# Multiplying the last experts' column factors into their weights, the final norm's products on VectorE, and holding one weight fetch behind the first gather

## The chip, the cores and the metric

The kernel runs on one core of one Trainium2 chip, in one launch. The metric is the device time of that launch in microseconds. A program on one core has one span: from its first to its last instruction. TensorE is called PE here, VectorE DVE, ScalarE ACT, GpSimd POOL; SP is the engine that issues most of the DMAs. Each of them works its own queue of instructions strictly in the order that was fixed when the kernel was built.

## The reference, cut to what matters

One layer of a hybrid backbone on 1024 tokens of width 1024, then a final RMSNorm. What bears on the change is its end, the mixture of 16 experts and the norm:

```python
x = x + mod_l[2] * token_mixer_out(zl, lat_grid, lp, ml_l)
x = x + mod_l[5] * hier_moe(modulate(rmsnorm(x, norm2_w[l]), mod_l[3], mod_l[4]), lp)
...
return rmsnorm(x, norm_f_w)

def hier_moe(h, lp):            # top-1 group of 4, then top-2 experts inside it
    ...
    hg = jnp.einsum("nd,edh->neh", t, lp["moe_w_gate"])
    hu = jnp.einsum("nd,edh->neh", t, lp["moe_w_up"])
    a = jax.nn.silu(hg) * hu * combine[..., None].astype(t.dtype)
    return jnp.einsum("neh,ehd->nd", a, lp["moe_w_down"]).reshape(B, L, D)
```

Each token goes to two of the 16 experts with a weight for each, and the sum of the two outputs is multiplied, column by column, by `mod_l[5]`, which is one row of 1024 factors for all tokens.

## The kernel before

**Stage out.** For each tile t of 128 tokens, `product` makes the mixer's output on PE and adds it to the residual, `transpose` and `logits` make the router's logits, `norm(t)` (L1580 to L1586) scales the tile's rows by their root mean square on ACT (L1584), adds the shift row on POOL (L1585) and writes the rows to `h2d` in DRAM; the last tile is done in two halves of 512 columns. `route` and `rank` are some twenty small DVE instructions per tile that end in the index lists `idx` (L1662) of each expert.

**Stage experts.** The jobs are the 16 experts, in a fixed order, `jobs[0]` to `jobs[15]`. For each: `exp_load` gathers the expert's rows in two halves of 112 by indirect DMAs on POOL's queue (L1672, 458 KB each); `exp_fetch` loads six weight tiles of 512 KB through SP's queue (four for gate and up, two for down); `exp_weights` splits each tile into a high part, cast on ACT (L1703), and a low part, subtracted on DVE or, for three tiles of the first job, on POOL (L1705); `exp_rows` or, for the first job, `exp_rows_first` transposes the rows on PE (L1721, L1738) and splits them (`split`, L215 on ACT and L216 on DVE); `exp_up` runs the products (three matmuls for each product of split parts, L230 to L232), then silu, the product with the up part (`a`, L1759) and its split (`ah`, `al`); `exp_down` runs the second products and evicts each half of 112 rows with one DVE instruction `y = p * weight * mod5` (L1777), where `weight` is the token's weight (gathered from `wd` in DRAM on POOL's queue, L1677) and `mod5` the row of column factors.

For the first 13 jobs y is added to `sum` in DRAM by an indirect DMA (L1681). The last three, the late ones, keep their sum on chip: `late_load` gathers their rows of `sum`, `exp_down` adds y (L1783), and `late` normalises the half (`late_norm`: squares, square root, reciprocal, then a product with the row `nf`) and scatters it to the output (L1681 again). All rows of `sum` are also read back (`rest_load`, eight tiles) and normalised by `rest_norm` for the tokens that no late expert touches: squares on ACT (L1900), an inverse square root by small DVE instructions on all eight tiles at once (L1902 and L1182 to L1187), then for tiles 0 to 3 one DVE instruction (L1907), and for tiles 4 to 7 a scale on ACT (L1909) and a product on POOL (L1910). `late` for job 13 also uses ACT and POOL (L1935, L1936), for jobs 14 and 15 DVE (L1934). The late scatters wait for all eight tiles of `rest_norm` to have been written, since they replace rows of these.

**The order.** A scheduler orders the instructions of each engine when the kernel is built, by the order in which the program states them and by its own estimate of when each is ready; `issue_after(i)` puts what follows behind instruction i on i's engine, `high_priority` ahead. In `stage_experts`, the casts of the first job stand behind `self.scaled`, the last ACT instruction of `norm`, and its DVE low parts behind `self.last`, the instruction that makes `idx`. A semaphore wait between queues is made by `sync_dep`. `rest_norm`'s DVE part stands behind `al` of job 14, `late` of job 13 behind the silu and `al` of job 15.

Of the kernel before, what the change touches and what calls it, by code (L numbers as in the profile page):

```python
# [8 lines left out]
F32 = mybir.dt.float32  # L9
F32R = mybir.dt.float32r  # L10
I32 = mybir.dt.int32
AF = mybir.ActivationFunctionType
ALU = mybir.AluOpType
# [17 lines left out]
HALF = CAP // 2  # L31
# [133 lines left out]
class Prog:  # L165
# [1289 lines left out]
    def stage_out(self):  # L1455
        nc = self.nc
# [25 lines left out]
        for dst, n, step, ch in ((self.ios, CAP, 1, 0), (tok, 8, 128, 1)):  # L1482
            i = self.t("O", "h", 2, I32, (128, n))
# [3 lines left out]
        i = self.t("O", "h", 2, F32, (128, 128))  # L1487
# [11 lines left out]
        gate, sh2, sc2 = (self.row_bc("O", f"row{i}", i) for i in (0, 1, 2))  # L1499
        self.x1 = []  # L1500
        for t in range(8):
            x = self.t("X", "x", 8)
# [4 lines left out]
        rs = self.t("O", "h", 2, F32, (128, 8, 20))  # L1507
# [3 lines left out]
        prep, rstd, sel = {}, {}, {}  # L1511

        def job(e):
            i = ORDER.index(e)
            k = i - NE + LATE
            extra = {} if k < 0 else dict(out=lambda h: self.oidx[:HALF, 2 * k + h:2 * k + h + 1],
                                                late=lambda h: self.yl[k * CAP + HALF * h:k * CAP + HALF * h + HALF, :])
            return dict(extra, e=e, pool="E", w=("X", "x", 8) if i % 2 else ("EW", "w", 6), n=HALF, halves=2, last=e == ORDER[-1],
                        idx=lambda h: self.idx[:, NE * h + e:NE * h + e + 1],
                        wgu=lambda i: A["w_gu"][e, i].rearrange("p k h -> p (k h)"),  # L1520
                        wdn=lambda k: A["w_dn"][e, :, k, :],
                        dst=lambda h: self.sidx[:HALF, NE * h + e:NE * h + e + 1])

        jobs = [job(e) for e in ORDER]
# [55 lines left out]
        def norm(t):  # L1580
            n = D if t < 7 else D // 2
            for a in range(0, D, n):
                h = hs[t][:, a:a + n]
                self.scaled = nc.scalar.activation(h, h, AF.Copy, scale=rstd[t])  # L1584
                nc.gpsimd.tensor_add(h, h, sh2[:, a:a + n])  # L1585
                nc.sync.dma_start(self.h2d[128 * t:128 * t + 128, a:a + n], h)  # L1586

        hs, ss, hT = {}, {}, {}
        split_m(0), split_m(1)
        for t in range(9):  # L1590
            if t < 8:
                product(t, 0)
            if t == 0:
                q = self.ps("ph", (128, 20))
# [93 lines left out]
            self.take(w[h], self.wd, j["idx"](h))  # L1688
        j["weight"] = lambda h: w[h][:, e:e + 1]

    def exp_fetch(self, j):
        j["m"] = [self.load(*j["w"], j["wgu"](i) if i < 4 else j["wdn"](i - 4)) for i in range(6)]

    def exp_weights(self, j, engines="vvvvvv", hi_after=None, lo_after=None):
        nc = self.nc
        pool = j["pool"]
        after = lambda i: self.tc.issue_after(i.ins) if i is not None else ExitStack()
        j["gu"], j["dn"], j["pins"] = [], [], []
        for i, m in enumerate(j["m"]):
            tag, bufs = ("g", 5) if i < 4 or i == 5 and j["last"] else ("d", 3)  # L1700
            mh, ml = (self.t(pool, tag + x, bufs, F32R, m.shape) for x in "hl")
            with after(hi_after):
                copied = nc.scalar.copy(mh, m)  # L1703
            with after(lo_after):
                lo = (nc.vector if engines[i] == "v" else nc.gpsimd).tensor_sub(ml, m, mh.bitcast(F32))  # L1705
            j["pins"].append((copied, lo))
            j["gu" if i < 4 else "dn"].append((mh, ml))
# [21 lines left out]
    def exp_rows_first(self, j):  # L1729

        n = j["n"]
        xh, xl = (self.t(j["pool"], x, 2, F32R, (128, 8, 2 * n)) for x in ("xh", "xl"))
        for h in range(2):
            p = self.ps("pb", (128, 2, 512))
            for q in range(2):
                for k in range(4):
                    kk = 4 * q + k
                    self.nc.tensor.transpose(p[:, q, n * k:n * k + n], j["rows"][h][:, 128 * kk:128 * kk + 128],  # L1738
                                             self.ident[:n, :n])
                s = slice(4 * q, 4 * q + 4), slice(n * h, n * h + n)  # L1740
                self.split(xh[:, s[0], s[1]], xl[:, s[0], s[1]], p[:, q, :4 * n].rearrange("p (k n) -> p k n", n=n))
        j["x"] = xh, xl

    def exp_up(self, j, between=None):
# [19 lines left out]
    def exp_down(self, j):  # L1764
        nc = self.nc
        pool, n, w = j["pool"], j["n"], j["n"] * j["halves"]
        ah, al = j["a"]
        j["y"] = []
        for h in range(j["halves"]):
            p = self.ps("pb", (128, 2, 512))  # L1770
            for k in range(2):
                for b in range(2):
                    s = slice(k * w + h * n, k * w + h * n + n)
                    c = slice(512 * b, 512 * b + 512)
                    self.mm3(p[:n, b, :], ah[:, s], al[:, s], j["dn"][k][0][:, c], j["dn"][k][1][:, c], k == 0, k == 1)
            y = self.t(*j["tags"][h])[:n] if "tags" in j else self.t(pool, "y", 2, F32, (n, D))
            nc.vector.scalar_tensor_tensor(y, p[:n].rearrange("p a b -> p (a b)"), j["weight"](h), self.mod5[:n],  # L1777
                                           op0=ALU.mult, op1=ALU.mult)
            j["y"].append(y)
            if "late" in j:  # L1780
                if "tags" not in j:
                    nc.sync.dma_start(j["late"](h), y)
                nc.vector.tensor_add(j["sum"][h], j["sum"][h], y)  # L1783
            elif self.in_loop:
                self.put(self.sum, j["dst"](h), y, compute_op=ALU.add)
            else:
                self.put_sum(j, h, y)
# [23 lines left out]
    def stage_experts(self):  # L1811
        nc = self.nc
# [8 lines left out]
        jobs = self.jobs  # L1821
# [8 lines left out]
        for e in range(NE):  # L1830
            if e + 2 < NE:
                self.exp_load(jobs[e + 2])
                self.exp_fetch(jobs[e + 2])

            between = {0: lambda: self.exp_rows(jobs[1]), NE - 3: lambda: self.exp_down(jobs[NE - 4]),
                       NE - 2: lambda: self.exp_down(jobs[NE - 3])}.get(e)
# [7 lines left out]
            if e == NE - 2:  # L1844
                with self.tc.issue_after(jobs[-1]["pins"][3][1].ins):
                    self.late_load(jobs[-2], "X", "x", 8)
                    self.late_load(jobs[-1], "X", "x", 8)
                self.rest_norm(jobs[-1]["pins"][2][0], jobs[-2]["silu"], jobs[-2]["al"])
            if e == NE - 1:
                with self.tc.issue_after(jobs[e]["silu"].ins), self.tc.issue_after(jobs[e]["al"].ins):  # L1850
                    self.late(jobs[-3], "gg")
                jobs[-2]["tags"] = (("X", "x", 8),) * 2
            if e and not between:
                self.exp_down(jobs[e - 1])
# [5 lines left out]
            if 4 <= e < 12:  # L1860
                t = e - 4
# [28 lines left out]
            self.after_puts(self.nc.sync.dma_start(x, self.sum[128 * t:128 * t + 128, :]))  # L1890
            self.xr.append(x)

    def rest_norm(self, act, act2, dve):

        nc = self.nc
        ss = self.t("V", "ss", 1, F32, (128, 8))
        for a, i in ((0, act), (4, act2)):
            with self.tc.issue_after(i.ins):
                for t in range(a, a + 4):
                    nc.scalar.activation(self.scratch, self.xr[t], AF.Square, accum_out=ss[:, t:t + 1])  # L1900
        with self.tc.issue_after(dve.ins):
            nc.vector.tensor_scalar(ss, ss, 1.0 / D, EPS, op0=ALU.mult, op1=ALU.add)  # L1902
            r = self.rsqrt("V", "rs", ss, 8)
            for t in (0, 4, 1, 5, 2, 6, 3, 7):
                x = self.xr[t]
                if t < 4:
                    nc.vector.scalar_tensor_tensor(x, x, r[:, t:t + 1], self.nf, op0=ALU.mult, op1=ALU.mult)  # L1907
                else:
                    nc.scalar.activation(x, x, AF.Copy, scale=r[:, t:t + 1])  # L1909
                    nc.gpsimd.tensor_mul(x, x, self.nf)  # L1910
                self.rest_out.append(nc.sync.dma_start(self.out[128 * t:128 * t + 128, :], x))

    def late(self, j, eng="vv"):
        for h in range(2):
            last = self.late_norm("E", HALF, j["sum"][h], self.scratch[:HALF], eng[h])
        with self.tc.issue_after(last.ins):
            for h in range(2):
                self.late_out(j["sum"][h], j["out"](h))
# [5 lines left out]
            self.after_puts(self.take(x, self.sum, j["idx"](h)))  # L1924
            j["sum"].append(x)

    def late_norm(self, pool, n, x, o, eng="v"):
        nc = self.nc
        r = self.t(pool, "r", 3, F32, (n, 1))
        nc.scalar.activation(o, x, AF.Square, accum_out=r)  # L1930
        nc.scalar.activation(r, r, AF.Sqrt, bias=self.eps[:n], scale=1.0 / D)
        nc.vector.reciprocal(r, r)
        if eng == "v":
            return nc.vector.scalar_tensor_tensor(x, x, r, self.nf[:n], op0=ALU.mult, op1=ALU.mult)  # L1934
        nc.scalar.activation(x, x, AF.Copy, scale=r)  # L1935
        return nc.gpsimd.tensor_mul(x, x, self.nf[:n])  # L1936

    def late_out(self, x, idx):
        i = self.put(self.out, idx, x)
# [195 lines left out]
```

## Time and profile before

| | us |
|---|---|
| median of 3 runs (lowest, highest) | 1715.55 (1713.96, 1719.74) |
| the profiled execution, whole time | 1713.86 |
| its span | 1712.1 |
| PE busy in the span | 1573.3 |
| DVE, ACT, POOL busy | 1194.5, 680.2, 333.6 |

A timeline row gives the start in us from the span's start, the duration in us, the engine, the line, the operation, what it writes and reads, the count of merged instructions, and in brackets how long the engine had been idle before and what ended that. The matmuls' ends are modelled, so a busy PE is not PE at its peak.

### The profile page before, as it was taken

Reading aid. Unit: us, or ns where it says so; the run is one execution under the profiler, and the core shown is the slowest. Engines: PE = TensorE matmul, PEld = TensorE weight load, DVE = VectorE, ACT = ScalarE, POOL = GpSimd, SP = SyncE. Lnnn points to the kernel's source line nnn. Section 1 sums busy time; section 2 is a strip of 40 time slices with the busy share of each in tenths; the row PEclk is TensorE's granted clock in tenths of the full one; section 3 lists DMA queues with packets and bytes.
Section 4 is the critical chain, followed back from the end, with each engine's and each line's share of the span. In section 5 each row is a group of like instructions: output and inputs, shape, how many; then the busy total and the mean of one; then the engine's idle time right before and its main releaser. Section 6 shows DMA issues by size and latency. Waiting matters only on the chain. (4 is left out here: it accounts for less than half of the span.)

```text
span 1712.1 us, 22676 instructions
## 1 busy us (share of the span) xinstructions
PE 1573.3 (92%) x8473; PEld 1300.0 (76%) x8473; DVE 1194.5 (70%) x1831; ACT 680.2 (40%) x1029; POOL 333.6 (19%) x288
## 2 busy tenths in 40 slices
PE   3999999699999999999999888899999969999992
PEld 1477777588877877888788777778888869999991
DVE  5678776898996437888643998864255467777766
ACT  4464555343330123444424433232133354544553
POOL 0000000000000001000001300026623354565636
PEclk9999999899999999999999999999999979999996
DMA  7533466222244436777443532486563389999974
GB/s 266 173 125 134 172 243 221 105 83 97 92 143 189 157 117 201 261 241 267 165 161 110 164 104 94 163 302 202 170 223 112 135 242 248 312 282 287 268 210 164
DMA packets 124355, 317.03 MB, mean 185 GB/s; under 512 B 18009, under 2 KB 40529, under 8 KB 124242
## 3 DMA queue, kind: packets, MB, share of 16 engines
q1 hardware_dynamic: 111562, 278.72, 47.2%
q0 software_dynamic: 10496, 32.36, 7.8%
q10 hardware_dynamic: 2184, 4.47, 0.7%
q8 instruction: 68, 1.11, 0.3%
q14 instruction: 45, 0.37, 0.1%
HBM read 226.49 MB, written 89.01 MB: 184 GB/s over the span
## 5 line engine op out<-in xcount | busy, mean ns | idle before, releaser
L230 PE MATMUL gp<-ht,wh 128*128 128x512 f32 x784 | 310.9, 397 | 17.9 <-ACT z L708 17.6
L232 PE MATMUL gp<-ht,wl 128*128 128x512 f32 x784 | 310.8, 396 | 0.0
L231 PE MATMUL gp<-ht,wh 128*128 128x512 f32 x784 | 309.8, 395 | 0.0
L230 PEld LDWEIGHTS gp<-ht,wh 128*128 128x128 f32 x784 | 148.7, 190 | 51.6 <-ACT z L708 18.4
L232 PEld LDWEIGHTS gp<-ht,wl 128*128 128x128 f32 x784 | 148.7, 190 | 32.2 <-issue 2.2
L231 PEld LDWEIGHTS gp<-ht,wh 128*128 128x128 f32 x784 | 148.5, 189 | 31.6 <-issue 1.2
L230 PE MATMUL pb<-xh,gh 128*128 128x224 f32 x512 | 142.5, 278 | 0.0
L231 PE MATMUL pb<-xl,gh 128*128 128x224 f32 x512 | 141.6, 277 | 0.0
L232 PE MATMUL pb<-xh,gl 128*128 128x224 f32 x512 | 141.0, 275 | 0.0
L723 DVE SCALAR_TENSOR_TENSOR u<-z,hy_cw,u 128x945 f32<-128x945 f32 (+2 forms) x96 | 115.3, 1221 | 3.6 <-ACT u L715 1.6
L215 ACT CAST wh<-w 128x1024 fp32r<-128x1024 f32 x57 | 59.8, 1050 | 138.5 <-PE gp L231 95.5
L230 PEld LDWEIGHTS pb<-xh,gh 128*128 128x128 f32 x512 | 99.3, 194 | 0.3 <-ACT xh L215 0.2
L231 PEld LDWEIGHTS pb<-xl,gh 128*128 128x128 f32 x512 | 99.3, 194 | 0.1
L232 PEld LDWEIGHTS pb<-xh,gl 128*128 128x128 f32 x512 | 99.3, 194 | 0.0
L216 DVE TENSOR_TENSOR wl<-w,wh 128x1024 fp32r<-128x1024 f32 x57 | 71.1, 1248 | 39.3 <-ACT wh L215 39.2
L723 DVE SCALAR_TENSOR_TENSOR u<-z,ml_cw,u 128x945 f32<-128x945 f32 (+2 forms) x64 | 77.7, 1221 | 3.8 <-ACT u L715 2.4
L216 POOL TENSOR_TENSOR ml<-m,mh 128x512 fp32r<-128x512 f32 x24 | 35.6, 1484 | 191.2 <-ACT mh L215 187.7
L708 ACT ACTIVATE z<-gp,bh 128x512 f32<-128x512 f32 x46 | 31.5, 685 | 100.1 <-PE gp L232 91.7
L864 POOL MEMSET z<- 128x1024 f32 x1 | 1.0, 962 | 312.2 <-DVE u L723 312.2
L1705 DVE TENSOR_TENSOR gl<-x,gh 128x1024 fp32r<-128x1024 f32 x33 | 40.8, 1240 | 29.9 <-ACT gh L1703 29.9
L1681 POOL DMA_INDIRECT sum<-y,sidx x26 | 42.9, 1650 | 79.4 <-DVE y L1777 76.1
L1444 DVE SCALAR_TENSOR_TENSOR g<-g,pb 128x1024 f32<-128x1024 f32 x16 | 19.5, 1221 | 53.9 <-PE pb L232 53.9
(610 smaller groups left out, 4011.2 us busy)
## 6 DMA issues: line engine op xcount, KB each, us to landing
w<-in_ada_rest SPq DMA_DIRECT2D x32, 512.0 KB
w<-in_w_gu SPq DMA_DIRECT2D x32, 512.0 KB
x<-in_w_gu SPq DMA_DIRECT2D x32, 512.0 KB
w<-in_w_gate SPq DMA_DIRECT2D x24, 512.0 KB
g<-gd SPq DMA_DIRECT2D x24, 512.0 KB
gd<-z SPq DMA_DIRECT2D x23, 512.0 KB
r<-in_ada_in SPq DMA_DIRECT2D x16, 512.0 KB
pd<-ft SPq DMA_DIRECT2D x32, 256.0 KB
```

Source lines behind the costliest of these rows:

```text
L215: self.copied = nc.scalar.copy(hi, src)
L216: return (nc.vector if eng == "v" else nc.gpsimd).tensor_sub(lo, src, hi.bitcast(F32))
L230: mm(ps, lh, rh, start=start, stop=False)
L231: mm(ps, lh, rl, start=False, stop=False)
L232: mm(ps, ll, rh, start=False, stop=stop)
L708: return lambda s, p: self.nc.scalar.activation(z[:, s], p, func, bias=bias, scale=scale)
L723: last = nc.vector.scalar_tensor_tensor(ui[:, r0:r1, c0:c1], zi[:, r0 + dy:r1 + dy, c0 + dx:c1 + dx], taps[:, i:i + 1], ui[:, r0:r1, c0:c1 ...
L864: nc.gpsimd.memset(zt, 0.0)
L1444: nc.vector.scalar_tensor_tensor(g, g, 1.0, p, op0=ALU.add, op1=ALU.mult)
L1681: return self.nc.gpsimd.indirect_dma_start(out=out, out_offset=bass.IndirectOffsetOnAxis(ap=ix, axis=0), in_=src, in_offset=None, **kw)
L1705: lo = (nc.vector if engines[i] == "v" else nc.gpsimd).tensor_sub(ml, m, mh.bitcast(F32))
```

## The change

It has two places.

At the end: the six down tiles of the three late jobs are multiplied by `mod5` on DVE before they are split, so that the eviction needs the token's weight alone. The sum is then updated straight from PSUM by one DVE instruction, `sum = p * weight + sum`, and y, which only the overflow path and `yl` need, is written by an ACT copy with a scale. `rest_norm` becomes two calls of four tiles each, with an inverse square root for each, and all eight products are DVE instructions; the first call's DVE part stands behind the low part of tile 4 of job 15, the second behind the last product of the first. `late_norm` has the DVE form alone. No POOL product is left there.

At the start of the experts: `norm(7)` becomes one DVE instruction per half instead of ACT and POOL, and `self.scaled` is not assigned for that tile. The six weight fetches of `jobs[2]` wait for `jobs[0]["in"]`, the last split of the first job's rows.

```diff
@@ stage_out, norm
-                self.scaled = nc.scalar.activation(h, h, AF.Copy, scale=rstd[t])
-                nc.gpsimd.tensor_add(h, h, sh2[:, a:a + n])
+                if t == 7:
+                    nc.vector.scalar_tensor_tensor(h, h, rstd[t], sh2[:, a:a + n], op0=ALU.mult, op1=ALU.add)
+                else:
+                    self.scaled = nc.scalar.activation(h, h, AF.Copy, scale=rstd[t])
+                    nc.gpsimd.tensor_add(h, h, sh2[:, a:a + n])
@@ exp_fetch, exp_weights, exp_rows_first
-    def exp_fetch(self, j):
-        j["m"] = [self.load(*j["w"], j["wgu"](i) if i < 4 else j["wdn"](i - 4)) for i in range(6)]
+    def exp_fetch(self, j, after=None):
+        j["m"] = []
+        for i in range(6):
+            m = self.t(*j["w"])
+            d = self.nc.sync.dma_start(m, j["wgu"](i) if i < 4 else j["wdn"](i - 4))
+            if after is not None:
+                self.sync_dep(d, after, "the first rows go ahead")
+            j["m"].append(m)
...
+            if "late" in j and i >= 4:
+                nc.vector.tensor_mul(m, m, self.mod5)
...
-                self.split(xh[:, s[0], s[1]], xl[:, s[0], s[1]], p[:, q, :4 * n].rearrange("p (k n) -> p k n", n=n))
+                j["in"] = self.split(xh[:, s[0], s[1]], xl[:, s[0], s[1]], p[:, q, :4 * n].rearrange("p (k n) -> p k n", n=n))
@@ exp_down
-            nc.vector.scalar_tensor_tensor(y, p[:n].rearrange("p a b -> p (a b)"), j["weight"](h), self.mod5[:n],
-                                           op0=ALU.mult, op1=ALU.mult)
...
             if "late" in j:
+                nc.vector.scalar_tensor_tensor(j["sum"][h], p, j["weight"](h), j["sum"][h], op0=ALU.mult, op1=ALU.add)
+                nc.scalar.activation(y, p, AF.Copy, scale=j["weight"](h))
                 if "tags" not in j:
                     nc.sync.dma_start(j["late"](h), y)
-                nc.vector.tensor_add(j["sum"][h], j["sum"][h], y)
@@ stage_experts
-                self.exp_fetch(jobs[e + 2])
+                self.exp_fetch(jobs[e + 2], None if e else jobs[0]["in"])
...
-                self.rest_norm(jobs[-1]["pins"][2][0], jobs[-2]["silu"], jobs[-2]["al"])
+                done = self.rest_norm(0, jobs[-1]["pins"][2][0], jobs[-1]["pins"][4][1])
+                self.rest_norm(4, jobs[-2]["silu"], done)
...
-                    self.late(jobs[-3], "gg")
+                    self.late(jobs[-3])
@@ rest_norm
+        with self.tc.issue_after(act.ins):
+            for i in range(4):
+                nc.scalar.activation(self.scratch, self.xr[a + i], AF.Square, accum_out=ss[:, i:i + 1])
         with self.tc.issue_after(dve.ins):
             nc.vector.tensor_scalar(ss, ss, 1.0 / D, EPS, op0=ALU.mult, op1=ALU.add)
+            r = self.rsqrt("V", f"rs{a}", ss, 4)
+            for i in range(4):
+                x, t = self.xr[a + i], a + i
+                last = nc.vector.scalar_tensor_tensor(x, x, r[:, i:i + 1], self.nf, op0=ALU.mult, op1=ALU.mult)
                 self.rest_out.append(nc.sync.dma_start(self.out[128 * t:128 * t + 128, :], x))
+        return last
```

## Rows read from the trace of the kernel before

**Rows 1.** Busy time by stretch: stretch, length, each engine (instructions), granted clock, DMA share, GB/s.
```profile
1350.00:1400.00 50.00, 32.50 (x196) 29.15 (x195) 27.64 (x76) 21.21 (x33) 23.85 (x15) 0.73 0.62 192
...
1550.00:1600.00 50.00, 50.00 (x383) 46.16 (x382) 35.79 (x37) 23.71 (x27) 29.15 (x22) 1.00 0.99 279
```
**Rows 2.** Waits from 1400 to 1670 us: who, for whom, total us, times, longest.
```profile
ACT gh L1703 <- DMA x<-in_w_gu: 1.6, 1, 1.6
```
**Rows 3.** Timeline of the experts' start: the gathers, SP's fetches, PE, DVE.
```profile
1375.76 1.26 POOL L1672 DMA_INDIRECT xg<-h2d,idx  x1 [4.40 <-DVE gmax L1959]
...
1377.94 7.01 SPq L220 DMA_DIRECT2D w<-in_w_gu  x4
...
1381.00 0.98 PE L1738 MATMUL pb<-ident,xg 112*128 112x112 f32 x4 [5.76 <-DMA xg<-h2d,idx]
1386.21 1.75 PE L1738 MATMUL pb<-ident,xg 112*128 112x112 f32 x8 [4.23 <-DMA xg<-h2d,idx]
...
1390.13 0.45 PE L1721 MATMUL pb<-ident,xg 112*128 112x112 f32 x1 [1.73 <-DMA xg<-h2d,idx]
...
1391.00 0.54 PE L231 MATMUL pb<-xl,gh 128*128 128x224 f32 x1
...
1390.22 0.61 DVE L216 TENSOR_TENSOR xl<-pb,xh 128x448 fp32r<-128x448 f32 x1
```
**Rows 4.** Timeline of POOL: two gathers issued while SP issues no weights.
```profile
1409.99 0.93 POOL L1672 DMA_INDIRECT xg<-h2d,idx  x1 [0.30 <-PE pb L232]
1411.23 1.27 POOL L1672 DMA_INDIRECT xg<-h2d,idx  x1 [0.31 <-issue]
```
**Rows 5.** DMA issues in the stretch of the second of these: count, us to landing.
```profile
xg<-h2d,idx POOLq DMA_INDIRECT x1, 7.1
```
**Rows 6.** Busy time by stretch, as in Rows 1: gathers with no weights beside them.
```profile
1411.00:1421.00 10.00, 10.00 (x76) 9.19 (x75) 9.62 (x30) 3.86 (x5) 3.13 (x3) 1.00 0.86 187
```
**Rows 7.** Timeline of the last tile's norm on POOL, the DVE's router, the first casts.
```profile
1368.87 2.49 POOL L1585 TENSOR_TENSOR h<-h,row 128x512 f32<-128x512 f32 x2 [1.07 <-ACT h L1584]
...
1368.97 0.24 DVE L1621 SCALAR_TENSOR_TENSOR logit<-ph,rstd,r_b 128x20 f32<-128x20 f32 x1 [0.99 <-PE ph L1574]
...
1370.28 1.19 DVE L1627 TENSOR_TENSOR rge<-rge,before 128x80 f32<-128x80 f32 x1
...
1369.32 3.87 ACT L1703 CAST gh<-w 128x1024 fp32r<-128x1024 f32 x4
```
**Rows 8.** Timeline: POOL's low parts, POOL's wait for `wd`, and PE's fourth expert's rows.
```profile
1384.55 4.66 POOL L1705 TENSOR_TENSOR dl<-w,dh 128x1024 fp32r<-128x1024 f32 x2
...
1404.10 1.69 POOL L1677 DMA_INDIRECT wt<-wd,idx  x1 [11.58 <-DMA wd<-dense]
...
1423.12 1.12 PE L1721 MATMUL pb<-ident,xg 112*128 112x112 f32 x10
```
**Rows 9.** Groups from 1660 to 1712 us, shapes apart: busy us, mean ns, idle before.
```profile
L1907 DVE SCALAR_TENSOR_TENSOR w<-w,rs,nf 128x1024 f32<-128x1024 f32 x2 | 6.6, 3363 | 0.0
...
L1783 DVE TENSOR_TENSOR x<-x,x 112x1024 f32<-112x1024 f32 x2 | 4.2, 2096 | 0.0
...
L1935 ACT ACTIVATE xg<-xg,r 112x1024 f32<-112x1024 f32 x2 | 2.3, 1150 | 0.3 <-DVE r L1932 0.2
```
**Rows 10.** Timeline of the end: DVE, then PE and POOL.
```profile
1658.07 2.35 DVE L1705 TENSOR_TENSOR gl<-x,gh 128x1024 fp32r<-128x1024 f32 x2
...
1666.37 0.17 DVE L1902 TENSOR_SCALAR ss<-ss 128x8 f32<-128x8 f32 x1 [3.12 <-ACT sq L1900]
...
1668.80 2.48 DVE L1907 SCALAR_TENSOR_TENSOR x<-x,rs,nf 128x1024 f32<-128x1024 f32 x2
...
1697.05 1.28 DVE L1934 SCALAR_TENSOR_TENSOR x<-x,r,nf 112x1024 f32<-112x1024 f32 x1
...
1679.02 0.77 PE L230 MATMUL pb<-dh,ah 128*112 128x512 f32 x1 [8.08 <-ACT ah L215]
...
1698.62 0.93 POOL L1681 DMA_INDIRECT out_dram<-x,oidx  x1 [0.70 <-DVEq L2078]
```

More of the change, by code (lines that the diff above doesn't have):

```diff
@@ L1776, in exp_down @@
             y = self.t(*j["tags"][h])[:n] if "tags" in j else self.t(pool, "y", 2, F32, (n, D))
-            nc.vector.scalar_tensor_tensor(y, p[:n].rearrange("p a b -> p (a b)"), j["weight"](h), self.mod5[:n],
-                                           op0=ALU.mult, op1=ALU.mult)
+            p = p[:n].rearrange("p a b -> p (a b)")
             j["y"].append(y)
             if "late" in j:
+                nc.vector.scalar_tensor_tensor(j["sum"][h], p, j["weight"](h), j["sum"][h], op0=ALU.mult, op1=ALU.add)
+                nc.scalar.activation(y, p, AF.Copy, scale=j["weight"](h))
                 if "tags" not in j:
                     nc.sync.dma_start(j["late"](h), y)
-                nc.vector.tensor_add(j["sum"][h], j["sum"][h], y)
-            elif self.in_loop:
+                continue
+            nc.vector.scalar_tensor_tensor(y, p, j["weight"](h), self.mod5[:n], op0=ALU.mult, op1=ALU.mult)
+            if self.in_loop:
                 self.put(self.sum, j["dst"](h), y, compute_op=ALU.add)
@@ L1891, in rest_load, with rest_norm, late @@
             self.xr.append(x)
-    def rest_norm(self, act, act2, dve):
+    def rest_norm(self, a, act, dve):
         nc = self.nc
[L1896 to L1900, printed above, removed]
+        ss = self.t("V", "ss", 2, F32, (128, 4))
+        with self.tc.issue_after(act.ins):
+            for i in range(4):
+                nc.scalar.activation(self.scratch, self.xr[a + i], AF.Square, accum_out=ss[:, i:i + 1])
         with self.tc.issue_after(dve.ins):
             nc.vector.tensor_scalar(ss, ss, 1.0 / D, EPS, op0=ALU.mult, op1=ALU.add)
[L1903 to L1910, printed above, removed]
+            r = self.rsqrt("V", f"rs{a}", ss, 4)
+            for i in range(4):
+                x, t = self.xr[a + i], a + i
+                last = nc.vector.scalar_tensor_tensor(x, x, r[:, i:i + 1], self.nf, op0=ALU.mult, op1=ALU.mult)
                 self.rest_out.append(nc.sync.dma_start(self.out[128 * t:128 * t + 128, :], x))
-    def late(self, j, eng="vv"):
+        return last
+    def late(self, j):
         for h in range(2):
-            last = self.late_norm("E", HALF, j["sum"][h], self.scratch[:HALF], eng[h])
+            last = self.late_norm("E", HALF, j["sum"][h], self.scratch[:HALF])
         with self.tc.issue_after(last.ins):
@@ L1925, in late_load, with late_norm @@
             j["sum"].append(x)
-    def late_norm(self, pool, n, x, o, eng="v"):
+    def late_norm(self, pool, n, x, o):
         nc = self.nc
@@ L1932, in late_norm @@
         nc.vector.reciprocal(r, r)
[L1933 to L1936, printed above, removed]
+        return nc.vector.scalar_tensor_tensor(x, x, r, self.nf[:n], op0=ALU.mult, op1=ALU.mult)
     def late_out(self, x, idx):
```

## The prediction

> **What bounds the kernel now.** I read the busy time by stretch first, then the waits, then the timelines of the two places where PE is not busy. In the middle of the experts PE is busy 50.00 of 50 us at the full clock [rows 1], and of all its feeders only one cast waits once for a weight DMA, for 1.6 us [rows 2]. So the middle is bound by PE: whatever is gained at the experts' start is handed on to the end unless a feeder comes late, and whatever DVE, ACT or POOL save in the middle is worth nothing. PE stands still at the experts' start, where it is busy 32.50 of 50 us at a mean granted clock of 0.73 [rows 1], and in the last 40 us, where it waits 8.08 us for `ah` of the last expert [rows 10]. The change touches just these two.
>
> At the start PE waits for rows. The first transposes start at 1381.00 when the first gather has landed, the next eight at 1386.21 when the second has [rows 3]. Then come ACT's and DVE's splits, of which the low part that the second matmul needs ends at 1390.22 + 0.61 = 1390.83; a transpose of the second expert that stands ahead in PE's queue waits for the third gather until 1390.13; the run of matmuls starts at 1391.00 [rows 3]. So there are two late things, 0.9 and 0.2 us before the start. Beside the gathers SP issues the third expert's weights from 1377.94 on [rows 3].
>
> At the end the span is led by DVE. It ends its last weight split at 1658.07 + 2.35 = 1660.42, and its last instruction at 1697.05 + 1.28 = 1698.33, 37.9 us on; 0.3 us later the last scatter is issued [rows 10]. From there to the span's end are 1712.1 - 1698.62 = 13.5 us, which the change does not touch. In this stretch two products of `rest_norm` took 3.36 us each beside POOL's products, against 2.48 / 2 = 1.24 us without them, and two additions took 2.10 us [rows 9, 10].
>
> **The end, part by part.** I add up what DVE has to do after the change from 1658.07 on, with 1.24 us [rows 10] for each instruction on 1024 columns, also for the new `sum = p * weight + sum`, whose nearest row that is.
> - the two weight low parts: 2.35 [rows 10];
> - `a` and `al` of job 14, and of job 15: 4 x 0.62 = 2.5, half the columns of the 1.24;
> - two inverse square roots, since `rest_norm` is now two calls: each as the one of before, 1668.80 - 1666.37 = 2.43 [rows 10], so 4.9;
> - 8 products of `rest_norm` and 6 of `late_norm`: 14 x 1.24 = 17.4. Four and two of them were POOL's;
> - 4 sums of jobs 14 and 15, in place of four evictions and four additions: 4 x 1.24 = 5.0;
> - 6 reciprocals at under 0.17 (a one-column instruction, as the 0.17 of rows 10): 1.0.
>
> Together 33.1, so 1691.2 if DVE never waits. The very last half must wait for its squares and square root on ACT; DVE has one product to do meanwhile, and I add 0.5: 1691.7 against 1698.33, a gain of 6.6 us. That DVE need not wait rests on three things. ACT is through with all eight squares at 1666.37 [rows 10]; I take it that the first four are done when the low parts are, so that the first call fills the 3.12 us that DVE stood idle there. `a` of job 15 then comes after the eight products, at 1658.07 + 2.35 + 1.2 + 4.9 + 9.9 = 1676.4, a little earlier than before, and PE's last product follows it with DVE still having job 13 and 14 to do. The scatters need the eight output writes: the last of these is issued some 6 us earlier than before, since POOL's products are gone.
>
> What is added elsewhere: six multiplications of down tiles by `mod5`, 6 x 1.24 = 7.4 us on DVE, before the split. DVE is busy 35.79 of 50 us in the middle [rows 1], so they cost nothing there; without that cover each would put 1.24 us ahead of a cast. For job 15 the two fall before 1658 into idle time; if they fell behind it, the end would be 2.5 us later. Six ACT copies of y at 1.15 [rows 9] lie beside DVE, with ACT free of four scales and two more of `late`; if the last two stood in front of the last squares, the end would be up to 2.3 us later. What is late next is DVE itself. Bounds: 9 us of gain if nothing waits and the low parts end 1 us earlier, since one addition in front of them is gone; 3 us if DVE keeps half of its former idle time and ACT's copies stand in the way. I take 6.6, from the count.
>
> **The start, part by part.** Holding SP's six fetches: SP would issue them at 1377.94 and now issues them after the last split of the first rows, about 12 us later. Behind them in SP's queue stands only what is issued after 1390. The rows of gathers without weights beside them: the second lands 1411.23 + 7.1 = 1418.3, which is 8.3 us after the first was issued at 1409.99 [rows 4, 5]. Before, the second was there 1386.21 - 1375.76 = 10.4 us after the first issue [rows 3]. So the second gather comes 2.1 us earlier, at 1384.1. Its splits follow with the same 4.6 us, which moves 1390.83 to 1388.7. The third gather, 458 KB more at 187 GB/s [rows 6], comes 2.5 us after, at 1386.6, and no longer holds PE. So matmuls start 2.1 us earlier. The Trainium skill, "DMA: Bandwidth & Descriptors", section "Queues, rings and completion order", says that each DMA engine takes turns between the queues it has work for; by that rule a gather alone would go twice as fast as beside SP's fetches, the 5.2 us from 1381.00 to 1386.21 would halve, and the gain would be 2.6. The rows of gathers alone are slower than that, and I go by them.
>
> The third expert's weights then arrive some 12 us later. The only cast that waited for a weight waited on an x tile [rows 2], and these are w tiles; 3.1 MB at 279 GB/s [rows 1] from 1390 on need 11 us, but they land one by one and are cast one by one, behind those of the second expert. I cost this at nothing; how large their margin was no row here shows, and without any it would be up to 10 us.
>
> The last tile's norm: POOL's 2.49 us go and DVE gets two instructions on 512 columns, 2 x 0.62 = 1.24. The DVE idles 0.99 us before the router's first instruction [rows 7], which hides one of them, and a router instruction on 80 columns that took 1.19 us beside POOL [rows 7] will be about 1 us shorter. The index may come between 1 us earlier and 0.6 us later. But `self.scaled` now stays at tile 6, so the scheduler may put the first expert's casts, 3.87 us for four [rows 7], ahead of the ACT instructions of the last router steps; each that slips in delays these by up to 1 us. I take zero for both together, with +-1.5.
>
> Sum: 6.6 + 2.1 = 8.7. The profiled execution took 1713.86, so 1705.2 by its own measure; the median of the runs is 1.7 above it, so I forecast **1706.9**.
>
> **The rivals.**
> 1. The start gives nothing. The casts come earlier, so POOL's three low parts, at 2.33 us each [rows 8], can be put ahead of the gathers in POOL's queue, where they stood behind; one or two of them in front take back the 2.1 us. For it: POOL is idle 4.4 us before the first gather [rows 3]. Against: the gathers have high priority. Time: 1715.55 - 6.6 = 1709.
> 2. The end gives half. If the order leaves DVE waiting for the ACT copies or the products of `rest_norm` stand in front of the late sums' own, 3 us remain: 1715.55 - 3 - 2.1 = 1710.5.
> 3. Slower than before. The late weights pile up in SP's DMA queue in front of `wd`. POOL waits for `wd` until 1404.10 [rows 8] and only then issues the fourth expert's gathers, which landed at 1418.3 against PE's use at 1423.12 [rows 4, 5, 8]. Of this margin of 4.8 us the earlier start eats 2.1. `wd` is issued at about 1394 with up to 2.5 MB ahead of it, so I expect it 2 to 3 us late, just within the margin of 2.7. Each us beyond this stalls PE by one; from 2.7 + 8.7 = 11.4 us on the change costs time, and at 17 us late it gives 1721. Against: the whole pile is 11 us.
> 4. The change doesn't move the start at all because the gathers wait on POOL's own work of issuing them: that is rival 1's time.
>
> **How the numbers follow.** The forecast case has 0.60 (1703 to 1709.5 with its own bounds), rival 1 with 4 together 0.21 (1707 to 1711.5), rival 2 0.13 (1709 to 1713.5), rival 3 0.06 (1716 to 1722). The range reaches from the best end, 9 + 4 below the median, to the half-gained cases: 1702 to 1713. About 0.3%, 5.1 us, is what a measurement of this kernel can tell from no change, so faster means under 1710.4: 0.59 of the forecast's 0.60, 0.14 of rival 1's, 0.04 of rival 2's, 0.77 in all. Within 0.3%: 0.18. Slower: 0.05.
>
> **What would show it.** In the trace of the changed kernel: the second gather's transposes at about 1384 and matmuls at about 1389; no weight fetch of SP between 1377 and 1387; PE's fourth expert's rows without idle time; no POOL product after 1660; every DVE instruction on 1024 columns at about 1.24 us; the last scatter some 8.7 us earlier. I am wrong if the last scatter moves but the start does not, if DVE has more than 2 us of idle time between 1660 and its last product, or if PE stands idle again between 1400 and 1640.

## The result, and the profile after

The changed kernel is slower: 1729.04 us (median of 5 runs) against 1713.96 for the kernel before beside it, ratio 1.0088, 95% interval 1.0067 to 1.0110. Forecast were 1706.9 us and a gain. Its profiled execution took 1727.15 us with a span of 1725.4, against 1713.86 and 1712.1 before: 13.3 us more.

The busy time by stretch of the changed kernel, in the columns of [rows 1] and with one stretch more, shows in one view where it goes:

```profile
1350.00:1400.00 50.00, 37.09 (x247) 33.80 (x247) 32.12 (x81) 22.84 (x34) 21.88 (x13) 0.80 0.55 184
1550.00:1600.00 50.00, 42.45 (x316) 39.30 (x315) 30.19 (x30) 19.25 (x23) 24.38 (x18) 0.93 0.81 216
1600.00:1650.00 50.00, 39.06 (x254) 34.89 (x253) 30.75 (x30) 17.65 (x21) 23.68 (x15) 0.86 0.69 177
```

The start is better than in [rows 1] (37.09 us of PE against 32.50, at 0.80 of the clock against 0.73). But the middle, where PE was busy 50.00 of 50 us, now has holes: 42.45 and 39.06. The granted clock falls with them, to 0.93 and 0.86, since PE comes back from each hole at the lower of its two levels, 1.2 GHz (granted 0.53 from 1586 to 1590, 0.50 from 1634 to 1640). The waits of the changed kernel from 1400 to 1700 us (who, for whom, total, times, longest) name the holes and what is behind them; none of these three pairs was there before:

```profile
DVE x L1711 <- DMA x<-in_w_dn: 21.5, 4, 7.8
DVE w L1711 <- DMA w<-in_w_dn: 4.6, 1, 4.6
PE pb L1732 <- DVE a L1770: 18.5, 2, 10.9
```

L1711 is the new multiplication of a down tile by `mod5`. DVE stands still for 26 us in all, because the tile is not there yet; PE stands still for 18.5 us because `a` (L1770, L1759 before) stands behind that in DVE's queue. The timeline of the first hole, rows of DVE, SP and PE:

```profile
1567.98 1.23 DVE L1716 TENSOR_TENSOR gl<-x,gh 128x1024 fp32r<-128x1024 f32 x1 [1.50 <-ACT gh L1714]
1577.03 1.23 DVE L1711 TENSOR_TENSOR x<-x,mod 128x1024 f32<-128x1024 f32 x1 [7.82 <-DMA x<-in_w_dn]
1578.17 1.22 DVE L1716 TENSOR_TENSOR gl<-x,gh 128x1024 fp32r<-128x1024 f32 x1
1583.22 1.23 DVE L1711 TENSOR_TENSOR x<-x,mod 128x1024 f32<-128x1024 f32 x1 [3.84 <-DMA x<-in_w_dn]
1584.37 1.22 DVE L1716 TENSOR_TENSOR gl<-w,gh 128x1024 fp32r<-128x1024 f32 x1
1585.50 0.62 DVE L1770 TENSOR_TENSOR a<-a,pb 128x448 f32<-128x448 f32 x1
...
1569.23 10.51 SPq L1698 DMA_DIRECT2D x<-in_w_dn  x2
...
1586.17 1.75 PE L1732 MATMUL pb<-ident,xg 112*128 112x112 f32 x8 [7.55 <-DVE a L1770]
```

SP issues the first of job 13's two down tiles at 1569.23; DVE has it at 1577.03. The row of SP reaches from the start of the first issue to the end of the second, and an issue lasts 0.33 us, so the second starts at 1569.23 + 10.51 - 0.33 = 1579.41, just behind the low part that ends at 1578.17 + 1.22 = 1579.39. That low part reads the x tile whose buffer the second fetch needs, and it stood behind the first multiplication. So the second multiplication waits for a fetch that had waited for the first multiplication. Before the change SP waited for DVE's low parts too: each of the pair starts right behind the low part that frees its buffer. But these low parts waited only 1.5 us for ACT's casts, and for no fetch, so the two issues started 2.73 us apart:

```profile
1573.69 1.23 DVE L1705 TENSOR_TENSOR gl<-x,gh 128x1024 fp32r<-128x1024 f32 x1 [1.50 <-ACT gh L1703]
1576.37 1.28 DVE L1705 TENSOR_TENSOR gl<-x,gh 128x1024 fp32r<-128x1024 f32 x1 [1.45 <-ACT gh L1703]
...
1574.94 3.06 SPq L220 DMA_DIRECT2D x<-in_w_dn  x2
...
1584.53 0.33 SPq L220 DMA_DIRECT2D w<-in_w_gu  x1
```

The second hole has three multiplications (DVE rows at 1616.00, 1625.51 and 1631.67 with 4.59, 6.01 and 3.80 us of wait) and costs PE 10.94 us.

**The balance of the two profiled executions.** SP's fetch of one tile of the tenth expert is at 1527.70 after and 1533.44 before: the stages up to there are 5.7 us ahead. The fetch of a w tile (1584.53 before, 1548.92 one round earlier, so 35.6 us for a round) is at 1589.07 after, 1543.19 one round earlier, 45.9 us: the first hole cost 10.3, 7.55 of it idle, the rest at the lower clock. The last expert's row transpositions:

```profile
1654.68 1.70 PE L1732 MATMUL pb<-ident,xg 112*128 112x112 f32 x16
```

```profile
1636.80 1.70 PE L1721 MATMUL pb<-ident,xg 112*128 112x112 f32 x16
```

They are 17.9 us later (the upper row is after, the lower before), so the second hole cost 17.9 + 5.7 - 10.3 = 13.3. From there to the last scatter the changed kernel needs 1713.08 - 1654.68 = 58.4 us, before 1698.62 - 1636.80 = 61.8 [rows 10]: 3.4 gained. The sum: -5.7 + 10.3 + 13.3 - 3.4 = 14.5, and the last scatter is 14.5 us later.

The tail of the changed kernel, rows of DVE, PE and POOL:

```profile
1678.59 2.48 DVE L1920 SCALAR_TENSOR_TENSOR x<-x,rs,nf 128x1024 f32<-128x1024 f32 x2
1682.18 1.22 DVE L1716 TENSOR_TENSOR gl<-x,gh 128x1024 fp32r<-128x1024 f32 x1
1689.13 0.17 DVE L1916 TENSOR_SCALAR ss<-ss 128x4 f32<-128x4 f32 x1 [1.61 <-ACT sq L1914]
1698.09 1.28 DVE L1792 SCALAR_TENSOR_TENSOR x<-pb,wt,x 112x1024 f32<-112x1024 f32 x1
1711.32 0.16 DVE L1943 RECIPROCAL r<-r 112x1 f32<-112x1 f32 x1 [1.15 <-ACT r L1942]
...
1683.45 0.37 PE L232 MATMUL pb<-xh,gl 128*128 128x224 f32 x1 [2.53 <-DVE gl L1716]
1697.57 0.77 PE L230 MATMUL pb<-dh,ah 128*112 128x512 f32 x1 [4.69 <-ACT ah L215]
...
1713.08 0.93 POOL L1684 DMA_INDIRECT out_dram<-x,oidx  x1 [1.70 <-DVEq L2086]
```

The products are as forecast (1.24 to 1.28 us each, the new sum 1.28, no POOL product). But the first call of `rest_norm` now stands ahead of job 15's last `gl`, for which PE waits 2.53 us, and DVE waits 1.61 us for squares in the second call and 1.15 in the last half.

### The profile page after: what moved, and what is told of

Its sections match the earlier page's. It is cut to its first block, busy times and chain, and to the rows that moved or that the text cites. A ratio compares the mean times of both kernels' runs of the same rounds, so it can differ in the third digit from the quotient of the medians.

```text
span 1725.4 us, 22675 instructions
## 1 busy us (share of the span) xinstructions
PE 1575.4 (91%) x8473; PEld 1301.1 (75%) x8473; DVE 1195.4 (69%) x1851; ACT 677.5 (39%) x1027; POOL 320.3 (19%) x280
## 5 line engine op out<-in xcount | busy, mean ns | idle before, releaser
L230 PE MATMUL gp<-ht,wh 128*128 128x512 f32 x784 | 311.1, 397 | 17.9 <-ACT z L708 17.5
```

The costliest lines, as they stand in the source:

```text
L230: mm(ps, lh, rh, start=start, stop=False)
```

## The experiments

All ratios are against runs of the kernel before on the same chip, with 95% intervals. **Queue theory**: the loss comes from the place of the multiplications in DVE's queue. **Rivals**: it comes from their work (7.4 us more on DVE), or from the held weights at the start.

**The start alone** (`e1_start`): the kernel before with the two edits at the start.

> The kernel before with the start of the change alone: the last tile's norm on VectorE and the third expert's weights held behind the first rows. Queue theory (the late multiplications, waiting in VectorE's queue for their weights, lose the time): the start's gain is handed on whole, 5.7 us as SP's fetches of the tenth expert are early in the trace of the changed kernel (1527.70 against 1533.44), so 1708.2 against 1714.0, ratio 0.9967, and PE stands idle nowhere between 1400 and 1640. Start theory (the held weights make everything behind them late, and the stalls at 1578 and 1624 follow from that): 1714 to 1725, with PE idle behind 1550. My prediction's own figure for the start: 2.1 us, 1711.9.

Measured: 0.9969 (0.9955 to 0.9982), a gain of 5.3 us, and no idle time of PE for DVE or a DMA between 1400 and 1640. The start theory of the loss falls.

**The end alone** (`e4_end`): the kernel before with all of the end's edits.

> The kernel before with the end of the change alone; the start is as before. Queue theory: the same stalls as in the changed kernel, without the start's gain: 1729.0 + 5.7 = 1734.7, ratio about 1.012. Start theory: no stalls, since no weights are held, and the tail's gain: 1708 to 1714.

Measured: 1.0105 (1.0082 to 1.0127); PE waits 8.18 us for `a` at 1593.66 and 9.94 at 1641.38. The stalls come with the end of the change and don't need the start.

**Without the multiplications** (`e2_nomul`):

```diff
-            if "late" in j and i >= 4:
-                nc.vector.tensor_mul(m, m, self.mod5)
```

> The changed kernel without the six multiplications of the late down tiles, so that the late experts' outputs lack the column factors. Queue theory: no stall behind 1550, the start's 5.7 us kept and the tail at least no longer than before; the tail from the last expert's second product on was 4.1 us shorter in the changed kernel (15.5 against 19.6), so 1704 to 1708, ratio 0.994 to 0.9965. Start theory: the stalls stay, 1720 or more. If the new order of the last norm is itself a loss, the time lies above that of the start alone.

Measured: 0.9962 (0.9948 to 0.9976). The six multiplications thus cost 1.0088 - 0.9962 = 1.26%, 21.6 us (with the two intervals, some 4 us to either side), with 7.4 us of work.

**The same multiplications, later** (`e3_mulpin`, then `e6_pin`): behind `al` of the expert before; in the second kernel none behind `al` of job 13, so that none falls into the tail.

```diff
             if "late" in j and i >= 4:
-                nc.vector.tensor_mul(m, m, self.mod5)
+                with after(mul_after):
+                    nc.vector.tensor_mul(m, m, self.mod5)
...
-                self.exp_weights(jobs[e + 1])
+                self.exp_weights(jobs[e + 1], mul_after=jobs[min(e, NE - 3)]["al"])
```

(`e3_mulpin` has `jobs[e]["al"]` in the last line.)

> The changed kernel with the same six multiplications, put behind the low part `al` of the expert before, so that the weights have long landed when VectorE comes to them. Queue theory (the place in the queue counts, not the work): within 3 us of the kernel without them, 1704 to 1710; two of them now stand in the tail, which may cost 2.5 us. Work theory (7.4 us more on VectorE in this stretch are what PE waits for): 7 us or more above the kernel without them. No wait of VectorE for a weight's DMA is left under the first.

> The changed kernel with the six multiplications put where the weights have landed and VectorE has time: job 13's behind `al` of job 12, those of jobs 14 and 15 behind `al` of job 13, so that none stands in the tail. Queue theory: as without them, ratio 0.995 to 0.9975 (without them 0.9962, with two of them in the tail 0.9981). Work theory: no better than 0.998.

Measured: 0.9981 (0.9966 to 0.9995) and 0.9957 (0.9940 to 0.9974). In the second kernel the middle is whole again, with all six multiplications in it, as the busy time by stretch and a row of DVE show:

```profile
1600.00:1650.00 50.00, 50.00 (x374) 45.55 (x373) 40.29 (x39) 26.54 (x32) 30.67 (x20) 1.00 0.88 226
...
1641.09 2.36 DVE L1712 TENSOR_TENSOR w<-w,mod 128x1024 f32<-128x1024 f32 x2
```

DVE is busy 40.29 of 50 us there (35.79 in [rows 1]), and PE 50.00. So the work costs nothing that can be told from noise (0.9957 with it, 0.9962 without), as I had said, and the place is what costs; the work theory falls. In `e3_mulpin` job 15's two multiplications stand in the tail and take 2.35 us there. That can be a part of its 2.4‰ more, but the intervals of the two kernels overlap.

**One pair back in its place** (`e7_job13`), and **one single multiplication back** (`e11_one`): job 13's, ahead of low parts that are due sooner.

```diff
-                self.exp_weights(jobs[e + 1], mul_after=jobs[min(e, NE - 3)]["al"])
+                self.exp_weights(jobs[e + 1], mul_after=jobs[min(e, NE - 3)]["al"] if e + 1 > NE - 3 else None)
```

```diff
-                with after(mul_after):
+                with after(mul_after if i == 5 or "first" not in j else None):
```

(In the second, `first` is set for job 13. The expectation below speaks of the last norm's order of `e5_best`, which has 0.9951; the kernel that ran has the order of `e6_pin`, from which it differs by this edit alone, so 0.9957 is what it is held against, and the ranges of the expectation move up by 0.6‰.)

> As the kernel with all six multiplications put late, but job 13's two stand again where the scheduler puts them by itself, ahead of low parts that are due sooner. Queue theory: one of the two stalls of the changed kernel comes back; there the first took 45.9 us from one fetch to the next of its kind against 35.6 before, so 10.3 us more than the kernel with all six late: ratio 1.001 to 1.004. PE idle for about 7.5 us near 1580 and nowhere else between 1420 and 1640. If a stall needs all six, or comes from the last pair alone: no loss.

> As the kernel with the six multiplications late and the last norm's first call behind `al` of job 14, but the first of job 13's two multiplications stands again where the scheduler puts it. If the stall is a loop (VectorE waits for a fetch, the low part behind it frees the buffer that the next fetch needs, and the next multiplication waits for that fetch), the loop is open with one: VectorE waits once, 7 to 9 us, the second fetch comes as late as in the trace of the changed kernel but nobody waits for it, and PE loses 8.4 - 5.1 = 3 us and its clock for a little: ratio 0.996 to 0.999. If each multiplication's own wait counts in full by itself, two thirds of 12 us: 0.9995 to 1.001.

Measured: 1.0030 (1.0013 to 1.0048), that is 0.73% or 12.5 us above `e6_pin`; and 0.9985 (0.9971 to 1.0000), 0.28% or 4.8 us above `e6_pin`. Rows of DVE, SP and PE of the first:

```profile
1585.98 1.23 DVE L1712 TENSOR_TENSOR x<-x,mod 128x1024 f32<-128x1024 f32 x1 [8.70 <-DMA x<-in_w_dn]
1587.12 1.22 DVE L1717 TENSOR_TENSOR gl<-x,gh 128x1024 fp32r<-128x1024 f32 x1
1592.17 1.23 DVE L1712 TENSOR_TENSOR x<-x,mod 128x1024 f32<-128x1024 f32 x1 [3.83 <-DMA x<-in_w_dn]
...
1577.31 11.39 SPq L1698 DMA_DIRECT2D x<-in_w_dn  x2
...
1595.12 1.75 PE L1733 MATMUL pb<-ident,xg 112*128 112x112 f32 x8 [8.43 <-DVE a L1771]
```

and of the second:

```profile
1585.58 1.23 DVE L1712 TENSOR_TENSOR x<-x,mod 128x1024 f32<-128x1024 f32 x1 [8.49 <-DMA x<-in_w_dn]
1586.72 1.22 DVE L1717 TENSOR_TENSOR gl<-x,gh 128x1024 fp32r<-128x1024 f32 x1
...
1577.12 11.18 SPq L1698 DMA_DIRECT2D x<-in_w_dn  x2
...
1589.66 0.99 PE L1733 MATMUL pb<-ident,xg 112*128 112x112 f32 x8 [3.16 <-DVE a L1771]
```

In both, SP's second fetch starts right behind the end of the low part that follows the first multiplication (1577.31 + 11.39 - 0.33 = 1588.37 behind 1588.34; 1577.12 + 11.18 - 0.33 = 1587.97 behind 1587.94). With one multiplication nobody waits for that fetch: PE's hole is 3.16 us in place of 8.43, and 8.43 less the 3.83 of wait and the 1.23 of work is 3.4. Two multiplications cost 12.5 us, one 4.8, with about 4 us of uncertainty on each. It is these rows that show the loop; the times agree with it, but only just: 0.9985 lies in the moved range for the loop, 0.9966 to 0.9996, and its interval ends at 1.0000, where the moved range for separate waits begins (1.0001).

**The last norm's order** (`e5_best`): as `e6_pin`, and

```diff
-                done = self.rest_norm(0, jobs[-1]["pins"][2][0], jobs[-1]["pins"][4][1])
+                done = self.rest_norm(0, jobs[-1]["pins"][2][0], jobs[-2]["al"])
```

> As the kernel with all six multiplications put late, and in addition the first call of the last norm stands behind `al` of job 14, as it did before the change, and not in front of job 15's weight parts. Tail theory: in the changed kernel without multiplications PE waited 3.0 us for a `gl` behind these products, and VectorE stood idle for 4.3 us between the first product and the last, part of it for squares that ACT had not made; with the order of before 2 to 3 us of that go, so 2 to 3 us below the kernel with six late multiplications, ratio 0.994 to 0.996. Rival (VectorE's count alone sets the end): the same time as that kernel, within 1 us.

Measured: 0.9951 (0.9936 to 0.9966), 0.6‰ or 1 us below `e6_pin`. PE's wait for `gl` is gone from its trace, and the way from the middle of the last expert's row transpositions to the last scatter is 55.9 us against 57.4 (61.2 and 60.5 in the two profiles of the kernel before; the middle is 0.6 us behind the start from which 61.8 was counted above). But 1 us is within both intervals: whether this order pays is not settled. Both kernels are faster than the one before and the changed one; this is the best that was run.

**The end without its stalls** (`e12_endpin`): `e5_best` with the start of before.

> The end of the change alone, with the six multiplications late and the first call of the last norm behind `al` of job 14; the start as before. My prediction's count for the end: 6.6 us, ratio 0.9961. By the trace of the changed kernel's relatives the last scatter comes 3 to 5 us earlier after the last expert's rows than before (61.2 us before, 57.4 and 55.9 in the two with late multiplications): ratio 0.997 to 0.9985.

Measured: 0.9965 (0.9952 to 0.9979), 6.0 us. In its trace that way to the last scatter is 56.7 us, 4.5 and 3.8 less than in the two profiles of before. My count of 6.6 lies within the interval; the range that I had read off the traces, 0.997 to 0.9985, was too low a gain. The start alone gave 5.3 us and the end alone 6.0, both together in `e5_best` 8.4; the intervals are too wide to say whether they add up.

**The parts of the start** (`e9_hold`, `e10_norm`): the hold alone, the norm's move alone.

> The kernel before with the hold alone: the third expert's six weight fetches wait for the first rows' last split. If the hold is the whole of the start's gain: first products 10.4 us after the first gather is issued (15.2 before), and the ratio of the start as a whole, 0.9955 to 0.998. My prediction gave the hold 2.1 us, 0.9988. What may take some of it back: PE's waits for nothing that the profile shows, near 1410 to 1417; in six profiles with held weights the stretch from the first products to a fetch of the tenth expert took 142.3 to 149.5 us, in three without 142.5 to 145.2.

> The kernel before with the last tile's norm alone moved to VectorE. My prediction: 0 +- 1.5 us, ratio 0.999 to 1.001, with the time from the last router product to the first gather unchanged (7.2 us before, 7.5 in most kernels with it). Rival: the first expert's casts, no longer behind that tile's ACT instruction, come earlier and let the first products start earlier; then ratio under 0.9985 and the first products under 15.2 us from the first gather.

Measured: 1.0006 (0.9991 to 1.0020) and 1.0008 (0.9996 to 1.0021). Neither gives anything that can be told from noise, and together they give 5.3 us (3.1 to 7.7). Rows of the hold alone, of POOL, DVE and PE:

```profile
1386.72 4.70 POOL L1711 TENSOR_TENSOR dl<-w,dh 128x1024 fp32r<-128x1024 f32 x2
...
1387.88 4.62 DVE L1711 TENSOR_TENSOR gl<-x,gh 128x1024 fp32r<-128x1024 f32 x1 [0.32 <-ACT gh L1709]
1392.43 1.14 DVE L216 TENSOR_TENSOR xl<-pb,xh 128x448 fp32r<-128x448 f32 x2
...
1385.33 1.76 PE L1744 MATMUL pb<-ident,xg 112*128 112x112 f32 x8 [1.46 <-DMA xg<-h2d,idx]
1393.63 0.56 PE L231 MATMUL pb<-xl,gh 128*128 128x224 f32 x1 [2.27 <-DVE xl L216]
```

The second gather's transpositions are early (7.4 us after the first gather's issue at 1377.92, against 10.45 before), but on DVE a low part of the second expert stands ahead of the first rows' last two `xl`, and beside POOL's low parts it takes 4.62 us in place of 1.22. PE gets `xl` only at 1393.63. That wait of 2.27 us takes back half of what the hold had won: the first products start 10.6 us after the first gather's issue, 15.2 before. Where the other half goes the rows don't show. The norm's move changes the order in which the scheduler puts the casts, and with them the low parts on DVE and POOL: in `e1_start` all four `xl` are ahead.

**The hold with that order mended** (`e13_holdorder`):

```diff
-                self.exp_weights(jobs[e + 1])
+                self.exp_weights(jobs[e + 1], lo_after=None if e else jobs[0]["in"])
```

> The kernel before with the hold alone, as in the run that gained nothing, and the second expert's low parts on VectorE put behind the last low part of the first rows. In that run a low part of the second expert stood ahead of the first rows' last two on VectorE and took 4.62 us beside POOL's low parts; PE then waited 2.27 us for the `xl` behind it. If that place is what the hold alone lacked, and the norm's move only happened to change it: first products run through from 10.3 to 11 us after the first gather is issued, ratio 0.996 to 0.998. If the move of the norm brings its part in another way (an earlier index, ACT free): no gain again, 0.999 to 1.002.

Measured: 1.0020 (1.0003 to 1.0037): no gain. The `xl` are early as expected (the run of matmuls starts 10.8 us after the first gather's issue), but another feeder is then late. Rows of POOL and PE:

```profile
1385.84 4.70 POOL L1711 TENSOR_TENSOR dl<-w,dh 128x1024 fp32r<-128x1024 f32 x2
1390.69 1.73 POOL L1672 DMA_INDIRECT xg<-h2d,idx  x1 [0.16 <-issue]
...
1406.14 0.94 POOL L1677 DMA_INDIRECT wt<-wd,idx  x1 [12.48 <-DMA wd<-dense]
...
1404.46 1.66 PE L1727 MATMUL pb<-ident,xg 112*128 112x112 f32 x15 [1.49 <-DMA xg<-h2d,idx]
1426.73 2.38 PE L1727 MATMUL pb<-ident,xg 112*128 112x112 f32 x15 [4.28 <-DMA xg<-h2d,idx]
```

Two low parts stand ahead of the third expert's gather on POOL (in `e1_start` one gather is between them, at 1389.24), `wd` comes at 1406.14, and PE waits 1.49 us for the third expert's rows and 4.28 for the fourth's: the latter is my third rival, with its place, in this kernel. So the place of the second expert's low parts was one thing that the hold alone lacked. That POOL's order is a second is read from the trace; no run changes it by itself.

**The kernel before once more** (`e8_same`), for a second profile.

> The kernel before once more, unchanged, for a second profiled execution. In the profiles of four kernels PE waited 1.5 to 4.4 us for nothing that the profile shows between 1405 and 1420, in those of before and after the change it did not. If these waits belong to the held weights, there is none here and the execution takes 1713 to 1715. If they come and go whatever the kernel, there is one here with a time of 1717 to 1721, or the next profile of a kernel with held weights has none.

Measured: 1712.79 us, with such waits, though short ones. Rows of PE:

```profile
1409.66 0.26 PE L231 MATMUL pb<-xl,gh 128*128 128x224 f32 x1 [0.81 <-issue]
1410.39 0.26 PE L231 MATMUL pb<-xl,gh 128*128 128x224 f32 x1 [0.24 <-issue]
1411.09 0.27 PE L232 MATMUL pb<-xh,gl 128*128 128x224 f32 x1 [0.44 <-issue]
```

They are not the change's. That they make an execution 5 us longer is not borne out: this one was short.

## Why the prediction was wrong, and where it was right

**The step that failed** is the sentence on the six multiplications: "DVE is busy 35.79 of 50 us in the middle [rows 1], so they cost nothing there; without that cover each would put 1.24 us ahead of a cast". I priced the work and looked for cover for the work. The cover was there (PE 50.00 of 50 with all six in the middle of `e6_pin`). What I left out is that each multiplication adds a wait, for its tile's DMA, to a queue that is worked strictly in order; that the scheduler was free to put it early there; that `gl` and `a`, for which PE waits, and the low part that frees the buffer of the next fetch stand behind it. The ACT cast that used to be the first reader of the tile came some 30 us after the fetch (a w tile that SP fetches at 1569.05 is cast at 1601.43 in the trace of before), so the view that shows no wait in the middle [rows 2] shows only that the old readers were late enough. The cost was 21.6 us, nearly three times the work. The Trainium skill, "PSUM — Partial Sum Buffer", section "Engine vs sequencer instructions", says that VectorE's queue is strictly first in, first out; the trace agrees: 26 us of DVE's standing still, nearly all of it with a low part behind whose cast was done (that of the low part at 1578.17 ended at 1570.63).

**None of my rivals was this one.** The third was the same kind of mechanism (an engine that waits for a DMA with something needed behind it), but at POOL and the fourth expert's rows. It did not happen in the changed kernel and did in `e13_holdorder`. Nor did any rival's time reach the measured one: the slowest was 1722. I closed with what would show me wrong, "if PE stands idle again between 1400 and 1640", and that is how it came.

**The end** was right in its count: the same instructions took 32.3 us of DVE's time in the tail of `e2_nomul` against 33.1 counted (its sums 1.28 against 1.24). Its idle time was mis-sized, 4.3 us against 0.5: I took the first four squares to be enough (and had named more than 2 us of idle time as a sign of being wrong), while the second call waits for its own, 1.61 us, the last half 1.15, and the splits' hand-overs to ACT two times 0.63. That the first call's new place would stand ahead of `gl` and hold PE I had not seen. With the order of before and the multiplications out of the way the end gave 6.0 us (3.6 to 8.2) against 6.6.

**The start** gave 5.3 us, not 2.1. Two terms are mis-sized, the second gather and the splits behind it. I bounded the gather by a gather without weights beside it that landed 8.3 us after the issue of the one before [rows 4, 5], behind four small gathers on the same queue. The rows of the changed kernel, of POOL and PE, and one of DVE in the kernel before:

```profile
1374.95 1.15 POOL L1675 DMA_INDIRECT xg<-h2d,idx  x1 [7.76 <-DVE rank L2003]
...
1379.64 0.98 PE L1749 MATMUL pb<-ident,xg 112*128 112x112 f32 x4 [6.00 <-DMA xg<-h2d,idx]
1381.73 1.75 PE L1749 MATMUL pb<-ident,xg 112*128 112x112 f32 x8 [1.11 <-DMA xg<-h2d,idx]
1385.44 0.54 PE L231 MATMUL pb<-xl,gh 128*128 128x224 f32 x1
```

```profile
1388.77 1.53 DVE L1705 TENSOR_TENSOR gl<-x,gh 128x1024 fp32r<-128x1024 f32 x1 [0.32 <-ACT gh L1703]
```

The second transpositions come 6.8 us after the first gather's issue, 10.45 before: 3.7 earlier, not 2.1. From the first rows to the second it is 2.09 us, 5.21 before. The rule of the Trainium skill, "DMA: Bandwidth & Descriptors", section "Queues, rings and completion order", on turns between queues, which I had set aside, gave 2.6 and was nearer than my rows; the halving was even exceeded. The splits, which I took over with the same 4.6 us, are 1.0 us shorter: the second expert's low part of the last row stood ahead of the first rows' `xl` on DVE before, and stands behind all four after. Together the run of matmuls starts 10.5 us after the first gather's issue, 15.2 before. So the norm's move, which I costed at zero, is zero by itself but changes the order of the low parts on DVE and POOL, and only with it did the hold give something. Of the other zeros, that of the third expert's late weights is borne out: from 1385 to 1440 ACT waits for no weight in the changed kernel.

## What to carry to other kernels

An instruction that is added to an engine with time to spare is not free by its work alone: ask which DMA or engine it waits for, how long its input lay idle under its old first reader, and what stands behind it in the queue. Where the wait's end depends on something behind the wait (a buffer that a later instruction frees), each such instruction starts the next one's delay; pin it behind something that certainly comes after the landing. Two edits that give nothing each can give 5 us together (here one fed the bound engine sooner and the other changed the order on its feeders), so test them together and apart.

## What the runs showed that I had not expected

A DVE subtraction of 128x1024 took 4.62 us beside two POOL subtractions that ran at 2.35 each, and 1.22 alone. It ended at 1392.50, 1.1 us after the POOL pair: it looks stopped rather than slowed. In the kernel before and in `e13_holdorder` such a subtraction also ended 1.1 us after POOL's (1390.30 against 1389.21, 1391.63 against 1390.54). The Trainium skill, "Trainium Architecture — The Big Picture", section "What this means for kernel authors", calls the port that the two share an exclusive lock; the rows agree.

In 12 of the 15 profiles PE stands between 1408 and 1421 us for up to 1.2 us at a time with nothing that the profile shows to wait for ("issue"); not in the first profile of before, that of after and that of `e13_holdorder`. In `e1_start` the stretch from the first products to a fetch of the tenth expert was 4.2 us longer than in the profile of before, as much as the start had gained, though its timed runs kept the gain. What PE lacks there is open. A difference of 4 us between two single profiles is thus no evidence here; the ratios are.
